# Four small edits of order in an encoder block: fold splits, PSUM bank names, the queue of the residual stores, the place of two means

## The chip, the cores and the metric

The kernel runs on one core of a Trainium2 chip. The metric is device time in microseconds (us), the median of several executions. A core has TensorE (PE: matmuls into PSUM; PEld is its weight load), VectorE (DVE), ScalarE (ACT), GpSimd (POOL) and SyncE (SP), which run their own instruction queues in order and wait for one another by semaphores. Transfers (DMA) are issued from an engine's queue, here nearly all from SyncE's.

## The reference

One encoder block on 1040 positions (16 meta tokens and 1024 inputs), D = 1024, in float32:

```python
h = rmsnorm(h_res, g_mix_pre)
u_a, c_g, b_g, v_b, gate_logits = split(h @ w_in)
y_a = fourier_mix(u_a) @ w_fourier          # real part of a 2-D DFT, 4 groups of 128
y_b = (b_g * centred_dwconv(c_g * v_b)) @ w_conv_out
gates = sigmoid(gate_logits + b_gates)
merged = gates[0] * y_a + gates[1] * y_b
h_res = h_res + rmsnorm(merged @ w_out, g_mix_post)
h2 = rmsnorm(h_res, g_ffn_pre)
a, v = split(centred_dwconv(h2 @ w_up))     # 2 x 2816 columns
h_res = h_res + rmsnorm((gelu(a) * v) @ w_down, g_ffn_post)
return h_res[:, 16:]
```

## The kernel before

**Arithmetic.** Each float32 operand is split into a high part (a cast on ScalarE, L127) and a low part (a subtraction on VectorE, L128). A product is then three matmuls, hi x hi, hi x lo, lo x hi (`mm3`, L155 to L163). Most products are tiled as pairs (`Pair`, L272): two rows of weights times two halves of the sequence in seven products in place of eight, with sums and differences of the operands. The seven steps of a pair use four PSUM tiles a, b, c, d and a sum u in SBUF; step 5 ends with x12 = d + u, step 6 with x21 = c + u (both L144 on VectorE).

**Stages.** In order: the input projection (gates, then the convolution branch, whose last jobs have the tiles `B_a` to `B_d`); the DFT along positions (`pq`, L731: 240 matmuls in eight groups of 30, one per block of 128 channels); the rest of the DFT, the merge and its store to `merged_d`; the output projection `mo` with both norms, in four chunks of 258, 258, 258 and 256 positions; the up projection (`up_*`) with convolution and gate; the down projection (`dna`, `dnb`); the last norm.

**Folds.** The operand of pq, folded by symmetry, has been stored in DRAM as `fold_d`, eight blocks. `next_fold(kt)` (L643) loads block kt into a raw room (`SP.dma_start`, L647) and splits it into `u` tiles. Rooms are shared: blocks 0, 2 and 4 use the raw room "b11h", blocks 1, 3 and 5 "t1l", so block 4 can be loaded only when block 2 is split. Blocks 0 to 3 are fetched from hooks in the last job of the projection, after its steps 1, 2, 4 and 5. Blocks 4 to 7 follow after the stage, then the cosine and sine tables (`cosr`, `sinr`, L738, with casts `cosh`, `sinh`). pq's banks come free with the last job's x21. `yb_d` takes the two results t of that job (L581).

**Output projection.** `project(c, hooks)` makes the eight tiles of chunk c: 24 matmuls each, then a square (`sq_m`, L884) and a scaling (L933) on ScalarE that evict them. Hooks run after numbered tiles, counted from 0. For chunks 1 and 2 (L1160): after tile 1 `norm_a(c - 1)`, after tile 5 `load_merged(c + 1)` (`mr`), after tile 6 `mean_b(c - 1)` and `norm_b(c - 1)`. `norm_a` scales the previous chunk's h by its first norm, adds the residual loaded as `xr` (L951), squares h (`sq_h`, ScalarE), and stores h to `hres_d` (L958), 32 stores in all, which the last stage reads back. `mean_b` is one matmul with a matrix of ones (`ms_h`, L892); `norm_b` scales h in place for the feed-forward (L977) and splits it. For chunk 3 the order of the tiles and the hooks are others (L1162 on), and the up projection's first products (`early`, `plain`) are woven in; `plain.first` copies a product to `up_s` on ScalarE (L1026), and the early pieces of the up projection's weights are loaded as `up_0er` and `up_1er` (L200).

**Order.** There is no table of costs. Instructions come in program order, except that code in `with behind(x):` is placed after instruction x, and each engine keeps that order. PSUM in the down projection is a pool of eight banks; `A` (`dna`) and `B` (`dnb`) are four tiles each, named at L1262, and the first step writes A.

Of the kernel before, what the change touches and what calls it, by code (L numbers as in the profile page):

```python
# [86 lines left out]
def block_kernel(ctx, tc, xT, w_u, w_in, w_fa, w_fa2, w_fb, w_fb2, w_co, w_out, w_up, w_dn,  # L87
# [17 lines left out]
    hres_d = dram.tile([P, KT, NTM], F32, name="hres_d")  # L105
# [13 lines left out]
    V, S, SP = nc.vector, nc.scalar, nc.sync  # L119
# [4 lines left out]
    def split(hi, lo, src, scale=None, eng=V, copy=S.copy):  # L124

        if scale is None:
            a = copy(hi, src)  # L127
            b = eng.tensor_tensor(out=lo, in0=src, in1=hi.bitcast(F32), op=ALU.subtract)  # L128
        else:
            a = S.mul(hi, src, scale)  # L130
            b = V.scalar_tensor_tensor(
                out=lo, in0=src, scalar=scale, in1=hi.bitcast(F32), op0=ALU.mult, op1=ALU.subtract
            )
        return a.ins, b.ins

    def behind(*instructions):

        st = ExitStack()
        for i in instructions:
            st.enter_context(tc.issue_after(i))  # L140
        return st

    def add(out, a, b, eng=V):
        return eng.tensor_tensor(out=out, in0=a, in1=b, op=ALU.add).ins  # L144
# [111 lines left out]
    def whole(t):  # L256
        return t[:, PS0 : PS0 + NH]
# [14 lines left out]
    class Pair:  # L272
# [11 lines left out]
        def step(self, psum, i, w, x):  # L284
            n = self.name
            if i == 0:
                self.a = wtile(psum, f"{n}_a")
                product(self.a, w, x, True, True)
                self.u = self.sums()
                self.kept = S.copy(self.u, whole(self.a)).ins  # L290
            elif i == 1:
                self.d = wtile(psum, f"{n}_d")
                product(self.d, w, x, True, True, self.parts)
            elif i == 2:
                b = wtile(psum, f"{n}_b")
                product(b, w, x, True, True, self.parts)
                add(self.u, whole(b), self.u)
                self.x22 = self.dst(22)
                self.added = add(self.x22, whole(self.d), self.u)
            elif i == 3:  # L300
                self.c = wtile(psum, f"{n}_c")
                product(self.c, w, x, True, True)
                add(self.x22, whole(self.c), self.x22)
                self.done(22, self.x22)
            elif i == 4:
                product(self.a, w, x, False, True)
                self.done(11, whole(self.a))
            elif i == 5:
                product(self.d, w, x, False, True)
                x12 = self.dst(12)  # L310
                add(x12, whole(self.d), self.u)
                self.done(12, x12)
            else:
                product(self.c, w, x, False, True)
                x21 = self.dst(21)
                add(x21, whole(self.c), self.u)
                self.done(21, x21)
# [8 lines left out]
    def run_pairs(psum, jobs, acts, hooks={}, first=None):  # L326

        loads = {0: first}

        def start(n):  # L330
            if n < len(jobs):
                pair, srcs, steps = jobs[n]
                loads[n] = ring.pair(pair.name, *srcs, steps)

        if first is None:
            start(0)
        start(1)
        cur = list(loads[0])
        for n, (pair, _, steps) in enumerate(jobs):
            nxt = []  # L340
            for j, i in enumerate(steps):
                pair.step(psum, i, cur[j], acts[PIECES[i]])
                if i > 1 and n + 1 < len(jobs):
                    todo = -(-len(jobs[n + 1][2]) * (j + 1) // len(steps))
                    with behind(pair.added):
                        nxt += itertools.islice(loads[n + 1], todo - len(nxt))
                if (n, i) in hooks:
                    hooks[n, i]()
            cur = nxt
            start(n + 2)  # L350
# [241 lines left out]
    jobs = []  # L592
# [42 lines left out]
        ("b11h", "b11l", "t1h"), ("t1l", "t2h", "t2l"), ("b11h", "t3h", "t3l"), ("t1l", "b21h", "b21l"),  # L635
        ("b11h", "b22h", "b22l"), ("t1l", "b11l", "t1h"), ("t4h", "b21h", "b21l"), ("t4l", "b22h", "b22l"),
    )
    folded = []

    def room(tag, dt, name):  # L640
        return hxp.tile([P, 4 * NH], dt, tag=tag, name=name)

    def next_fold(kt):  # L643

        raw, hi, lo = (room(t, dt, f"u{kt}{i}") for i, (t, dt) in enumerate(zip(FOLD_ROOMS[kt], (F32, F32R, F32R))))
        w = FW + 512
        SP.dma_start(raw[:, :w], fold_d[kt])  # L647
        split(hi[:, :w], lo[:, :w], raw[:, :w])
        xs = [(hi[:, at : at + H], lo[:, at : at + H]) for at in (H, 0)]
        folded.append((xs, (hi[:, FW:w], lo[:, FW:w])))  # L650

    hooks = {(NE1 + kt, 3): lambda kt=kt: transformed(kt) for kt in range(KT)}
    for kt in range(KT):
        hooks[NE1 + kt, 5 if kt < KT - 1 else 0] = lambda kt=kt: fold(kt)
    hooks[len(jobs) - 1, 1] = lambda: next_fold(0)
    hooks[len(jobs) - 1, 2] = lambda: next_fold(1)
    hooks[len(jobs) - 1, 4] = lambda: next_fold(2)
    hooks[len(jobs) - 1, 5] = lambda: next_fold(3)
    run_pairs(psum, jobs, hx, first=job0, hooks=hooks)
    proj_s.close()  # L660


# [47 lines left out]
    def bank(name):  # L710
        return psum.tile([P, 512], F32, tag="bank", name=name)
# [5 lines left out]
    with ExitStack() as st:  # L717
# [37 lines left out]
        for i in range(NLT):  # L755
            n = _lrows(i)
# [49 lines left out]
    for f in range(KT):  # L806
# [41 lines left out]
        lo = TM - T0 + CHM[1][0]  # L848
# [46 lines left out]
    def load_merged(c):  # L895
        c0, n = CHM[c]
        v = valid(c)
        parts = []
        for k in range(0, KT, 3):
            e = min(k + 3, KT)  # L900
            t = ring.raw(f"mr{c}_{k}")[:, : (e - k) * n].rearrange("p (k n) -> p k n", n=n)
            SP.dma_start(t[:, :, :v], merged_d[:, k:e, c0 + TM - T0 : c0 + TM - T0 + v])
            if v < n:
                V.memset(t[:, :, v:], 0.0)
            parts += [merged_parts(c, kt, t[:, kt - k])[0] for kt in range(k, e)]
        merged[c] = parts
# [32 lines left out]
    def norm_a(c):  # L939
        c0, n = CHM[c]  # L940
        v = valid(c)
        ms = next(z[c])
        rr = np_.tile([P, W], F32, tag="rr", name=f"rr{c}", bufs=2)[:, :n]
        got = rsqrt_of(f"r2_{c}", scratch, ms, n, rr)
        sq = squares(f"h{c}", n)
        next(sq)
        xr = []
        for f in range(0, KT, 2):
            t = eo.tile([P, 2 * W], F32, tag="o", name=f"xr{c}_{f}", bufs=4)
            t = t.rearrange("p (f n) -> p f n", f=2)  # L950
            SP.dma_start(t[:, :, :v], xT[:, f : f + 2, TM + c0 : TM + c0 + v])  # L951
            xr += [t[:, i, :v] for i in range(2)]
        for f in range(KT):
            h = h_at(c, f)
            scaled = mul(h, h, rr).ins
            add(h[:, :v], h[:, :v], xr[f])
            sq.send(h)
            SP.dma_start(hres_d[:, f, c0 : c0 + v], h[:, :v])  # L958
        z[c] = sq
        return got, scaled  # L960

# [7 lines left out]
    def norm_b(c):  # L969
        c0, n = CHM[c]  # L970
        if c not in rs:
            inverse(c)
        rr = rs[c]
        A, B = second(c)
        for f in range(KT):
            h = h_at(c, f)
            V.scalar_tensor_tensor(out=h, in0=h, scalar=col("g_fpre", f), in1=rr, op0=ALU.mult, op1=ALU.mult)  # L977
            if c < 2:
                a, e = max(c0, 1), min(c0 + n, NH + 1)
                put(hx["b11" if f < 4 else "b21"], f % 4, hA[f // 4][:, f % 4, a:e], a - 1, e - a)  # L980
            elif f < 4:
                sub(A(f), h, A(f))
                put(hx["t1"], f, A(f), c0 - 513, n)
            else:
                put(hx["b22"], f - 4, B(f), c0 - 513, n)
# [16 lines left out]
    def mean_b(c):  # L1002
        z[c] = next(z[c])
# [153 lines left out]
    project(0, {4: new_banks, 5: lambda: load_merged(1)})  # L1157
    for c in range(1, 4):
        hooks = {
            1: lambda: norm_a(c - 1), 5: lambda: load_merged(c + 1), 6: lambda: (mean_b(c - 1), norm_b(c - 1)),  # L1160
        }
        order = range(KT)  # L1162
        if c == 3:
            order = (6, 7, 0, 1, 4, 5, 2, 3)
            hooks = {
                1: lambda: norm_a(2),
                3: lambda: plain.load(0, "t1h"),
                4: lambda: plain.load(1, "t1l"),
                5: lambda: first_blocks("t3h"),
                6: lambda: (mean_b(2), inverse(2)),  # L1170
                7: lambda: first_blocks("t3l"),
            }
        project(c, hooks, order)
# [63 lines left out]
    jobs = [ups[n] for n in ORDER]  # L1237
# [21 lines left out]
    z11, u, z22 = (fn.tile([P, 4, HALF], F32, name=n) for n in ("z11", "dn_u", "z22"))  # L1259
    zz = (z11, u), (z12, z22)  # L1260
    ssum = [fn.tile([P, HALF], F32, name=f"ss{i}") for i in range(2)]
    B, A = ([bank(f"dn{n}{f}") for f in range(4)] for n in "ba")  # L1262
    LATE = 4
    AHEAD = 3
    CUT = 256
# [233 lines left out]
```

## Time and profile before

| what | value |
| --- | --- |
| median of 3 runs | 1218.7 us (1218.63 to 1220.26) |
| the profiled execution | 1222.5 us |
| its span | 1220.7 us |
| mean granted TensorE clock in it | 0.986 |
| PE busy | 1186.2 us (97%) |
| DVE busy | 1001.6 us (82%) |
| ACT busy | 550.6 us (45%) |
| DMA moved | 184.01 MB, 151 GB/s in the mean |

Times in the trace are us from the start of the span. Busy time is the time in which an engine executes; issues of transfers, semaphores and branches are not counted. The chain that ended last is followed back from the last instruction, at each step to what released it. A wait is idle time of an engine ahead of an instruction, put down to what released it last. A row of the timeline gives start, duration, engine, line, operation, out<-in with shapes, count, and in brackets the idle time ahead of it. The profile names lines of the kernel before; in the changed kernel, lines below L660 stand 11 further down.

### The profile page before, as it was taken

To read this page: it belongs to the slowest core of one execution; us is meant where nothing else is said; L and a number is where in the kernel's file an instruction comes from. 1 tells how busy PE (TensorE), PEld (TensorE's weight loads), DVE (VectorE), ACT (ScalarE), POOL (GpSimd) and SP (SyncE) were. 2 spreads that over 40 slices of the span, in tenths; PEclk is the share of its full clock that TensorE was granted. 3 is DMA by queue.
4 is the path that set the end of the run, shared out by engine and by line. 5 is a ranking of instruction groups with operands and counts; after the bars stand their busy time and mean duration, and the time that the engine had idled before them with its cause. 6 is when DMAs were issued, how large, how long until landed. Compare 5 with 4: busy or idle time off the path is not lost.

```text
span 1220.7 us, 22312 instructions
## 1 busy us (share of the span) xinstructions
PE 1186.2 (97%) x8822; PEld 1143.0 (94%) x8822; DVE 1001.6 (82%) x1755; ACT 550.6 (45%) x999; POOL 0.4 (0%) x6
## 2 busy tenths in 40 slices
PE   8999999999999999998999999999999999999995
PEld 7999999999999999998999999999999988888884
DVE  8999876757488866989699999989988989766678
ACT  6743333323342344656545443444344434454562
POOL 0000000000000000000000000000000000000000
PEclk9999999999999999999999999999999999999998
DMA  6336554132876757465233334323222498354433
GB/s 248 122 111 219 196 174 165 61 130 85 258 226 216 250 168 116 127 112 152 96 120 123 112 132 147 122 96 130 96 78 87 146 318 313 95 164 121 132 128 138
DMA packets 78472, 184.01 MB, mean 151 GB/s; under 512 B 7934, under 2 KB 24910, under 8 KB 78368
## 3 DMA queue, kind: packets, MB, share of 16 engines
q1 hardware_dynamic: 78224, 182.47, 47.5%
q8 instruction: 69, 1.13, 0.4%
q14 instruction: 35, 0.29, 0.1%
q10 hardware_dynamic: 144, 0.12, 0.0%
HBM read 131.30 MB, written 51.26 MB: 150 GB/s over the span
## 4 chain that ended last, share of the span: by engine, by line
PE 75%; DVE 14%; DMA 7%; issue 2%; ACT 2%; SPq 0%; DVEq 0%; ACTq 0%
PE up_d L159 3%; PE up_d L163 3%; PE up_d L161 3%; PE up_c L161 3%; PE up_c L159 3%; PE dna L159 3%; PE up_c L163 3%; PE dna L161 3%; PE dna L163 3%; PE up_a L159 3%; PE up_a L163 3%; PE up_a L161 3%; PE pq L731 2%; PE dnb L163 2%; PE dnb L161 2%; PE dnb L159 2%
## 5 line engine op out<-in xcount | busy, mean ns | idle before, releaser
L159 PE MATMUL mo<-mh,wo 128*128 128x258 f32 (+1 forms) x256 | 73.9, 289 | 0.0
L163 PE MATMUL mo<-mh,wo 128*128 128x258 f32 (+1 forms) x256 | 73.1, 285 | 0.0
L161 PE MATMUL mo<-ml,wo 128*128 128x258 f32 (+1 forms) x256 | 72.9, 285 | 0.0
L159 PEld LDWEIGHTS mo<-mh,wo 128*128 128x128 f32 x256 | 49.3, 192 | 0.2
L161 PEld LDWEIGHTS mo<-ml,wo 128*128 128x128 f32 x256 | 49.2, 192 | 0.2
L163 PEld LDWEIGHTS mo<-mh,wo 128*128 128x128 f32 x256 | 49.2, 192 | 0.0
L127 ACT CAST up_1h<-up_1t 128x512 fp32r<-128x512 f32 x11 | 6.8, 622 | 75.2 <-DVE up_1t L144 52.5
L1096 ACT ACTIVATE up_1o<-up_1x,pr 128x512 f32<-128x512 f32 x33 | 26.9, 816 | 27.9 <-DVE up_1x L144 27.5
L1100 ACT ACTIVATE up_0o<-up_0o 128x512 f32<-128x512 f32 x44 | 27.8, 631 | 24.1 <-DVE up_0o L1098 23.8
L159 PE MATMUL up_d<-b22h,up_5h 128*128 128x258 f32 (+1 forms) x168 | 34.0, 283 | 0.8 <-DVE up_1x L144 0.8
L163 PE MATMUL up_d<-b22h,up_5l 128*128 128x258 f32 (+1 forms) x168 | 34.2, 284 | 0.0
L161 PE MATMUL up_c<-t3l,up_3h 128*128 128x258 f32 (+1 forms) x168 | 34.1, 285 | 0.0
L163 PE MATMUL up_b<-t2h,up_2l 128*128 128x258 f32 (+1 forms) x168 | 34.0, 283 | 0.0
L161 PE MATMUL up_d<-b22l,up_5h 128*128 128x258 f32 (+1 forms) x168 | 33.9, 283 | 0.0
L161 PE MATMUL up_b<-t2l,up_2h 128*128 128x258 f32 (+1 forms) x168 | 33.9, 283 | 0.0
L159 PE MATMUL up_c<-t3h,up_3h 128*128 128x258 f32 (+1 forms) x168 | 33.8, 282 | 0.0
L159 PE MATMUL up_b<-t2h,up_2h 128*128 128x258 f32 (+1 forms) x168 | 33.8, 282 | 0.0
L159 PE MATMUL up_c<-t4h,up_6h 128*128 128x258 f32 (+1 forms) x168 | 33.8, 282 | 0.0
L159 PE MATMUL up_d<-t1h,up_1h 128*128 128x258 f32 (+1 forms) x168 | 33.7, 282 | 0.0
L163 PE MATMUL up_d<-t1h,up_1l 128*128 128x258 f32 (+1 forms) x168 | 33.7, 282 | 0.0
L163 PE MATMUL up_c<-t3h,up_3l 128*128 128x258 f32 (+1 forms) x168 | 33.6, 281 | 0.0
L161 PE MATMUL up_d<-t1l,up_1h 128*128 128x258 f32 (+1 forms) x168 | 33.6, 281 | 0.0
(1321 smaller groups left out, 4328.4 us busy)
## 6 DMA issues: line engine op xcount, KB each, us to landing
g<-gp_d SPq DMA_DIRECT2D x35, 512.0 KB
up_1r<-in_w_up_dram SPq DMA_DIRECT2D x22, 512.0 KB
gp_d<-up_0o SPq DMA_DIRECT2D x44, 256.0 KB
up_0r<-in_w_up_dram SPq DMA_DIRECT2D x20, 512.0 KB
s<-sig_d SPq DMA_DIRECT2D x16, 514.0 KB
sig_d<-g_s SPq DMA_DIRECT2D x30, 257.0 KB
u<-fold_d SPq DMA_DIRECT2D x8, 777.0 KB
fold_d<-fold SPq DMA_DIRECT2D x8, 521.0 KB
```

The lines of the kernel that those rows point to most:

```text
L127: a = copy(hi, src)
L159: nc.tensor.matmul(o, wh, h, start=first, stop=False, **kw)
L161: nc.tensor.matmul(o, wh, l, start=False, stop=False, **kw)
L163: newest[:] = [nc.tensor.matmul(o, wl, h, start=False, stop=last, **kw).ins]
L731: nc.tensor.matmul(o, a[:, s], b[:, ks], start=kt == n_ == ks.start == 0, stop=kt == KT - 1 and n_ == 2, skip_group_check=True,)
L1096: S.activation(t, ap[:, 1 : 1 + HALF], AF.Identity, bias=col("cb_ffn", b), scale=w(1))
L1100: S.activation(t, t, AF.Gelu_apprx_tanh)
```

## The change

Four edits.

```diff
@@ Pair.step
-                add(x12, whole(self.d), self.u)
+                self.freed = add(x12, whole(self.d), self.u)
@@ folds
-    def next_fold(kt):
+    def load_fold(kt):
...
         SP.dma_start(raw[:, :w], fold_d[kt])
-        split(hi[:, :w], lo[:, :w], raw[:, :w])
...
+        loaded.append((hi[:, :w], lo[:, :w], raw[:, :w]))
+
+    def split_fold(kt):
+        split(*loaded[kt])
+
+    def next_fold(kt):
+        load_fold(kt)
+        split_fold(kt)
...
-    hooks[len(jobs) - 1, 4] = lambda: next_fold(2)
-    hooks[len(jobs) - 1, 5] = lambda: next_fold(3)
+    for step, kt in ((1, 0), (2, 1), (4, 2)):
+        hooks[len(jobs) - 1, step] = lambda kt=kt: next_fold(kt) if kt < 2 else load_fold(kt)
+    hooks[len(jobs) - 1, 5] = lambda: load_fold(3)
     run_pairs(psum, jobs, hx, first=job0, hooks=hooks)
+    with behind(jobs[-1][0].freed):
+        split_fold(2)
+        split_fold(3)
@@ norm_a
-            SP.dma_start(hres_d[:, f, c0 : c0 + v], h[:, :v])
+            S.dma_start(hres_d[:, f, c0 : c0 + v], h[:, :v])
@@ hooks of chunks 1 and 2
-            1: ..., 5: ..., 6: lambda: (mean_b(c - 1), norm_b(c - 1)),
+            1: ..., 5: ..., 7: lambda: (mean_b(c - 1), norm_b(c - 1)),
@@ down projection
-    B, A = ([bank(f"dn{n}{f}") for f in range(4)] for n in "ba")
+    A, B = ([bank(f"dn{n}{f}") for f in range(4)] for n in "ab")
```

The hooks at 1 and 5 (`norm_a`, `load_merged`) stay. What the edits do to the engines' queues is seen at three places.

VectorE at the end of the input projection. `B_s` of B_d is x12, `B_s` of B_c is x21 (which frees pq's banks), the `u` rows are the splits of folds 2 and 3, the `t` rows products of the convolution branch. Before:

```order
409 L128 TENSOR_TENSOR u_3674<-u_3672,u_3673 128x1554
410 L144 TENSOR_TENSOR B_s_3702<-B_d,B_u 128x514
411 L150 TENSOR_TENSOR t_0_3491<-B_s_3702,t_0_3491 128x514
412 L128 TENSOR_TENSOR u_3707<-u_3705,u_3706 128x1554
413 L144 TENSOR_TENSOR B_s_3735<-B_c,B_u 128x514
414 L150 TENSOR_TENSOR t_1_3492<-B_s_3735,t_1_3492 128x514
```

And now:

```order
409 L144 TENSOR_TENSOR B_s_3700<-B_d,B_u 128x514
410 L128 TENSOR_TENSOR u_3674<-u_3672,u_3673 128x1554
411 L150 TENSOR_TENSOR t_0_3491<-B_s_3700,t_0_3491 128x514
412 L144 TENSOR_TENSOR B_s_3731<-B_c,B_u 128x514
413 L128 TENSOR_TENSOR u_3705<-u_3703,u_3704 128x1554
414 L150 TENSOR_TENSOR t_1_3492<-B_s_3731,t_1_3492 128x514
```

Each of the two adds now stands ahead of a split that it stood behind. On SyncE, the store of the second t (`yb_d<-t_1`) now stands ahead of the load of fold 5, behind which it stood.

ScalarE in the output projection of chunk 2, where `norm_a(1)` squares h of chunk 1. Before:

```order
341 L884 ACTIVATE sq_h_3_5539<-hA_5136 128x258 [waits DVE_49,Activation_49]
342 L884 ACTIVATE sq_h_4_5545<-hA_5137 128x258 [waits DVE_49,Activation_49]
343 L884 ACTIVATE sq_h_5_5551<-hA_5137 128x258 [waits DVE_49,Activation_49]
344 L884 ACTIVATE sq_h_6_5557<-hA_5137 128x258 [waits DVE_49,Activation_49]
345 L884 ACTIVATE sq_h_7_5563<-hA_5137 128x258 [waits DVE_49,Activation_49]
346 L884 ACTIVATE sq_m_2_5592<-mo_2_5567 128x258 [waits DVE_49,PE_49]
347 L933 ACTIVATE hA_5136<-mo_2_5567,pr 128x258
```

And now:

```order
346 L895 ACTIVATE sq_h_4_5545<-hA_5137 128x258 [waits DVE_49,Activation_49]
347 L969 DMA hres_d<-hA_5137 128x258 [waits DMAHW7_49]
348 L895 ACTIVATE sq_h_5_5551<-hA_5137 128x258 [waits DVE_49,Activation_49]
349 L969 DMA hres_d<-hA_5137 128x258 [waits DMAHW1_49]
350 L895 ACTIVATE sq_h_6_5557<-hA_5137 128x258 [waits DVE_49,Activation_49]
351 L969 DMA hres_d<-hA_5137 128x258 [waits DMAHW2_49]
352 L895 ACTIVATE sq_h_7_5563<-hA_5137 128x258 [waits DVE_49,Activation_49]
353 L969 DMA hres_d<-hA_5137 128x258 [waits DMAHW4_49]
354 L895 ACTIVATE sq_m_2_5592<-mo_2_5567 128x258 [waits DVE_49,PE_49]
355 L944 ACTIVATE hA_5136<-mo_2_5567,pr 128x258
```

A store stands behind each square, and some of them wait for an earlier transfer's semaphore, ahead of the evictions of the next tiles (`sq_m` and the scaling).

TensorE where the down projection begins, the last row of the up projection and the first of `dna`. Before:

```order
7756 L163 MATMUL up_1_c<-t4h,up_1_6l 128x256
7757 L159 MATMUL dna_12181<-gd_0h,wd_0h 128x512 [waits DVE_49,Activation_49]
7758 L161 MATMUL dna_12181<-gd_0l,wd_0h 128x512
7759 L163 MATMUL dna_12181<-gd_0h,wd_0l 128x512
7760 L159 MATMUL dna_12182<-gd_0h,wd_0h 128x512
```

And now:

```order
7756 L163 MATMUL up_1_c<-t4h,up_1_6l 128x256
7757 L159 MATMUL dna_12177<-gd_0h,wd_0h 128x512 [waits DVE_49,Activation_49]
7758 L161 MATMUL dna_12177<-gd_0l,wd_0h 128x512
7759 L163 MATMUL dna_12177<-gd_0h,wd_0l 128x512
7760 L159 MATMUL dna_12178<-gd_0h,wd_0h 128x512
```

Nothing moves there but the numbers of the tiles; the first row waits for VectorE in both. The matmul of the mean, `ms_h` of chunks 0 and 1, stands 24 rows later on TensorE than before, at the end of the eighth tile instead of the seventh.

More of the change, by code (lines that the diff above doesn't have):

```diff
@@ L637, in block_kernel @@
     )
-    folded = []
+    folded, loaded = [], []
     def room(tag, dt, name):
         return hxp.tile([P, 4 * NH], dt, tag=tag, name=name)
-    def next_fold(kt):
+    def load_fold(kt):
         raw, hi, lo = (room(t, dt, f"u{kt}{i}") for i, (t, dt) in enumerate(zip(FOLD_ROOMS[kt], (F32, F32R, F32R))))
@@ L654, in block_kernel @@
         hooks[NE1 + kt, 5 if kt < KT - 1 else 0] = lambda kt=kt: fold(kt)
-    hooks[len(jobs) - 1, 1] = lambda: next_fold(0)
-    hooks[len(jobs) - 1, 2] = lambda: next_fold(1)
-    hooks[len(jobs) - 1, 4] = lambda: next_fold(2)
-    hooks[len(jobs) - 1, 5] = lambda: next_fold(3)
+    for step, kt in ((1, 0), (2, 1), (4, 2)):
+        hooks[len(jobs) - 1, step] = lambda kt=kt: next_fold(kt) if kt < 2 else load_fold(kt)
+    hooks[len(jobs) - 1, 5] = lambda: load_fold(3)
     run_pairs(psum, jobs, hx, first=job0, hooks=hooks)
+    with behind(jobs[-1][0].freed):
+        split_fold(2)
+        split_fold(3)
     proj_s.close()
@@ L1159, in block_kernel @@
         hooks = {
-            1: lambda: norm_a(c - 1), 5: lambda: load_merged(c + 1), 6: lambda: (mean_b(c - 1), norm_b(c - 1)),
+            1: lambda: norm_a(c - 1), 5: lambda: load_merged(c + 1), 7: lambda: (mean_b(c - 1), norm_b(c - 1)),
         }
```

## The prediction

> **What bounds the kernel now.** I read the profile's page first: busy times, then the chain that ended last by engine.
>
> ```profile
> span 1220.7 us, 22312 instructions
> PE 1186.2 (97%) x8822; PEld 1143.0 (94%) x8822; DVE 1001.6 (82%) x1755; ACT 550.6 (45%) x999; POOL 0.4 (0%) x6
> PE 75%; DVE 14%; DMA 7%; issue 2%; ACT 2%; SPq 0%; DVEq 0%; ACTq 0%
> ```
>
> TensorE is busy for 1186.2 of 1220.7 us, and no edit here removes a matmul. So all that the change can give lies in TensorE's waits and in the time that its clock is held down. The waits, by what ended them, come next (total, times, longest):
>
> ```profile
> PE up_a L159 <- ACT up_u L290: 2.9, 2, 1.9
> PE dna L159 <- DVE up_1x L144: 2.7, 1, 2.7
> PE ms_h L892 <- DVE sq_h L144: 2.4, 1, 2.4
> PE up_z L159 <- ACT up_s L1026: 2.2, 1, 2.2
> PE pq L731 <- DVE B_s L144: 2.1, 1, 2.1
> ```
>
> Each of the four edits points at one of these rows: fold at pq, banks at dna, mean at ms_h, stores at the two rows of the up projection. I then cut the stretches around the waits into windows of 3.41 us and read the granted clock (PEclk):
>
> ```profile
> 312.65:316.06 3.41, 1.28 (x11) 1.24 (x11) 2.86 (x4) 1.49 (x1) 0.00 (x0) 1.00 0.97 304
> 316.06:319.47 3.41, 3.41 (x18) 3.41 (x17) 1.67 (x1) 0.00 (x0) 0.00 (x0) 0.50 0.92 311
> ...
> 575.47:578.88 3.41, 1.55 (x13) 1.35 (x13) 3.38 (x10) 2.76 (x6) 0.00 (x0) 1.00 0.01 4
> 578.88:582.29 3.41, 3.41 (x19) 3.41 (x18) 2.52 (x4) 1.76 (x3) 0.00 (x0) 0.50 0.21 75
> ...
> 991.90:995.31 3.41, 3.38 (x8) 2.73 (x9) 3.41 (x6) 0.73 (x1) 0.00 (x0) 0.50 0.86 315
> ```
>
> The columns are the window, its length, busy time of PE, PEld, DVE, ACT, POOL, the clock, DMA share, GB/s. A window in which TensorE was busy for 1.28 or 1.55 us is followed by one at half clock, worth 3.41 x 0.50 = 1.7 us of work lost. After a shorter wait that does not happen:
>
> ```profile
> 554.98:558.39 3.41, 2.33 (x18) 1.00 0.91 172
> 558.39:561.80 3.41, 2.73 (x23) 1.00 0.51 196
> ```
>
> (only TensorE's busy time here): with 2.33 us busy the next window keeps its clock. So a wait of some 2 us costs about 3.8 us here, and a wait of about 1 us costs only itself. The Trainium skill ("TensorE: Matmul & The Clock Gate", the quick table at its end) asks for no idle gaps over about 3 us; this trace shows half clock after gaps of 1.9 to 2.1 us, so I go by the trace; by the page's figure no gap here would be punished and each edit would be worth its wait alone.
>
> **Fold.** Around the start of pq, in the chain and on VectorE, SyncE's and ScalarE's queues:
>
> ```profile
> 314.85 30.45 PE pq L731 x240
> ...
> 308.24 1.78 DVE L128 TENSOR_TENSOR u<-u,u 128x1554 fp32r<-128x1554 f32 x1 [0.53 <-ACT u L127]
> 309.94 0.69 DVE L144 TENSOR_TENSOR B_s<-B_d,B_u 128x514 f32<-128x514 f32 x1
> 310.66 0.70 DVE L150 TENSOR_TENSOR t<-B_s,t 128x514 f32<-128x514 f32 x1
> 312.32 1.78 DVE L128 TENSOR_TENSOR u<-u,u 128x1554 fp32r<-128x1554 f32 x1 [0.97 <-ACT u L127]
> 315.95 1.78 DVE L128 TENSOR_TENSOR u<-u,u 128x1554 fp32r<-128x1554 f32 x1 [0.51 <-ACT u L127]
> 335.83 1.78 DVE L128 TENSOR_TENSOR u<-u,u 128x1554 fp32r<-128x1554 f32 x1 [1.81 <-ACT u L127]
> ```
>
> ```profile
> 312.33 0.40 PE L163 MATMUL B_c<-t4h,B_6l 128*128 128x258 f32 x2
> ```
>
> The last product ends at 312.73. The add that frees its bank stands behind the split of fold 3 (312.32 to 314.10), so pq starts at 314.85. After the change the add for x12 (309.94, 0.69) comes first, then the split of fold 2 (1.78, to 312.4), the product with t (0.70) and the freeing add (0.69 like its sister): 312.4 + 1.4 = 313.8, or some 0.1 less, since such operations overlap by that much at 309.94. TensorE then starts at about 313.75. The start gains 1.1 us, the remaining gap is 1.0 us, and by the rows above the half-clock window goes too: 1.1 + 1.7 = 2.8 us off, if nothing is late behind it.
>
> Something is. The split of fold 2 now ends at 312.4 instead of 310.0, and its raw room is where fold 4 is loaded. Each load waits in SyncE's queue in order:
>
> ```profile
> 314.13 0.32 SPq L647 DMA_DIRECT2D u<-fold_d  x1
> 317.75 0.73 SPq L738 DMA_DIRECT2D cosr<-in_cos_dram  x1
> ```
>
> cosr goes out at 317.75, right after the split of fold 4 has ended (315.95 + 1.78 = 317.73). A fold 4 loaded 2.3 us later moves this to about 320.0. One store of yb is also now ahead of the load of fold 5 and waits for the second product with t, which stands behind the split of fold 3. ScalarE takes the cosines first:
>
> ```profile
> 330.69 1.50 ACT L127 CAST cosh<-cosr 105x1566 fp32r<-105x1566 f32 x1 [8.83 <-DMA cosr<-in_cos_dram]
> 334.31 2.88 ACT L127 CAST u<-u 128x1554 fp32r<-128x1554 f32 x2
> ```
>
> It idles 8.83 us for cosr, and folds 6 and 7 are cast only after it. pq is eight groups of 30 matmuls; (30.45 - 1.7) / 8 = 3.6 us each. Group 6 began at about 314.85 + 30.45 - 2 x 3.6 = 338.1, and its split ended at 335.83 + 1.78 = 337.6: only 0.5 us of slack. TensorE, 2.8 us earlier, wants group 6 at 335.3. If cosr lands as before, the split holds it to 337.6, a gain of 0.5. If cosr lands 1.2 us (the transfers are bound by the 0.92 to 0.97 DMA share of the windows above, and catch up) to 2.3 us later (they don't), group 6 starts at 338.8 to 339.9, a loss of 0.7 to 1.8; and TensorE's gap there, 2.3 to 4.6 us, may cost another half-clock window, 1.7. Bounds: -0.5 to +3.5. I take the middle, **+1.5**. Without the delay behind it the term would be -2.8.
>
> **Banks.** The chain at the start of the down projection:
>
> ```profile
> 991.18 0.61 DVE up_1x L144
> 991.93 0.76 PE dna L159
> ```
>
> The first dna product waits 2.7 us for the last up_1x add, which reads the bank that the product will write. Swapping the two lists looks as if it gave A other banks. But the banks are handed out when a tile is first written, not when it is named, and A is written first in both programs; in the order of the changed kernel the first dna product waits for VectorE as before. So **0**; both bounds are 0, and the half-clock window at 991.90 stays.
>
> **Stores and mean.** The chain from 478 to 578 is one of VectorE, ScalarE and transfers; TensorE has slack in it. These rows of the chain, and the waits:
>
> ```profile
> 477.97 8.52 DMA mr<-merged_d
> ...
> 499.44 5.52 DMA hres_d<-hA
> ...
> 525.10 15.55 DMA hres_d<-hB
> 540.67 0.49 DVE hB L977
> ...
> 551.73 7.11 DMA up_1er<-in_w_up_dram
> ```
>
> ```profile
> 540.67 0.49 DVE L977 SCALAR_TENSOR_TENSOR hB<-hB,pr,rrb 128x258 f32<-128x258 f32 x1 [3.06 <-DMA hres_d<-hB]
> ```
>
> ```profile
> 544.85 6.34 SPq L958 DMA_DIRECT2D hres_d<-hB  x8
> 551.29 0.38 SPq L1076 DMA_DIRECT2D early_d<-up_1e  x1
> 551.73 0.44 SPq L200 DMA_DIRECT2D up_1er<-in_w_up_dram  x1
> ```
>
> Moving the mean of chunks 0 and 1 one tile later lets 24 matmuls of 0.12 us (3.6 / 30, the same width), 2.9 us, run into the 2.4 us wait of ms_h. That wait is not on the chain: TensorE waits again at the up projection (2.2 and 2.9 above), so time saved at 502 is idled away at 546 to 578. Worth 0 by itself.
>
> The stores leave SyncE's queue. There the last eight stand ahead of the weight load of 551.73, whose landing the chain needs: moved, the load goes out earlier, but still behind the early_d store that waits for ScalarE. Between 0 and -3.0; I take -1.5. VectorE's wait of 3.06 us at 540.67 is for a store to land before its tile is overwritten. The queue changes, the transfer engines don't. Between 0 and -3.06; I take half, -1.5. Against this, ScalarE issues 32 stores. The only issue on its queue now took:
>
> ```profile
> 0.73 0.41 ACTq L111 DMA_DIRECT2D pr<-in_par_dram  x1
> ```
>
> Eight a chunk at 0.41 are 3.3 us, between squares that come as fast as VectorE's adds, so most is hidden; but the copy of up_s for which TensorE waited 2.2 us at the up projection now stands behind five such stores of chunk 3: 0 to +2. VectorE's scaling of chunk 0 (four operations, 1.7 us) also falls behind its wait for mr (8.52 above): 0 to +1.7. Together I take +0.5. Sum **-2.5**, bounds -6 to +4 (the upper end below, under the rival).
>
> The Trainium skill ("Trainium Kernel Development and Optimization", Key Constraints) says that transfers issued by several engines run on the same 16 DMA engines, and that this only saves issue time. By that rule the 3.06 us stay and the term would be -1.0; no run here shows it yet.
>
> **Sum.** +1.5 + 0 - 2.5 = -1.0 us. The profiled execution took 1222.5 us with a span of 1220.7, 3.8 over the median of the runs, 1218.7; the difference is carried to the median: 1217.7.
>
> **Rivals.**
> 1. *The transfers come earlier* (0.36). Stores land sooner beside loads that no longer queue behind them, the 3.06 us at 540.67 and the load at 551.73 are saved in full (-6), and the fold yields between 0 and its -0.5: 1212 to 1214, with the half-clock window of 578.88 gone too 1211. For it: the chain names the transfers. Against: DMA share near full at these places.
> 2. *Slower: ScalarE is blocked by its stores* (0.28). In the changed order the later stores of a chunk wait for DMA semaphores (one for each of eight in rotation), among them those of the xr loads, and behind them stand the evictions of the out projection, a square and a scaling for each tile. If each of chunks 0 and 2 holds ScalarE for 2 us beyond what TensorE's slack covers, +4; with the fold at +1.5 that is 1224. It decides where a wait of a store exceeds the 2.2 us of slack at the next up_z. For it: the order shows the waits; the fold's bound of +3.5 alone, with the stores at 0, gives 1222. Against: ScalarE is busy only 45%.
> 3. *Every named wait goes with its half-clock window* (0.04): -2.8, -(2.7 + 1.7) for banks, -(2.4 + 1.7) for the mean, -3.06: 1204. Against: the order at dna and the slack of group 6.
> 4. *The change does not do what it says*: for the banks that is my forecast already.
>
> **Chances.** My forecast (-1.0, within about 2.4) has 0.32, the rest as above. A measurement of this kernel can tell about 0.2%, 2.4 us, from no change. Rivals 1 and 3 are faster by more, rival 2 slower: faster 0.40, same 0.32, slower 0.28. The range drops rival 3 and the outer parts of 1 and 2: 1211.5 to 1223.5. The forecast's own: 1216.3 to 1221.
>
> **What would show it.** Right: pq starts at 313.7 with a gap near 1.0 and full clock after it, but a new wait of pq on u before its seventh group, with cosr's cast later than 330.69; dna waits 2.7 us as before with half clock behind it; ms_h waits little and the up projection as much or nearly. Wrong: dna starts right after the last up product (banks did move), pq runs through without a wait (the fold is worth -2.8), or ScalarE's waits on DMA stand ahead of the evictions and TensorE waits for mo (rival 2).

## The result and the profile after

The changed kernel took 1227.95 us in the median of 4 runs (1226.38 to 1229.44) against 1218.66 us of the kernel before (1217.15 to 1220.26): ratio 1.0079, 95% interval 1.0063 to 1.0096, so 9.3 us slower. Timed again in another session the ratio was 1.0063 (1.0041 to 1.0086). The forecast was 1217.7, the range 1211.5 to 1223.5. The kernel before itself lies at 1213.6 to 1218.7 in different sessions; so only ratios within a session are compared below, and a ratio is turned into us with 1215.

The page of the changed kernel's profiled execution:

```profile
span 1224.4 us, 22290 instructions
PE 1185.4 (97%) x8822; PEld 1140.8 (93%) x8822; DVE 1002.0 (82%) x1755; ACT 551.0 (45%) x999; POOL 0.4 (0%) x6
PE 74%; DVE 15%; DMA 6%; issue 2%; ACT 2%; SPq 0%; DVEq 0%; ACTq 0%
```

Busy times are as before; the loss is in waits. This execution took 1226.4 us and the profiled one of the kernel before 1222.5, 3.8 over that kernel's median, so the two traces lie only 3.9 us apart and a second trace of each is used below. TensorE's waits (total, times, longest):

```profile
PE up_z L159 <- ACT hB L944: 3.1, 1, 3.1
PE dna L159 <- DVE up_1x L144: 2.6, 1, 2.6
...
PE mo L159 <- ACT mh L127: 1.9, 1, 1.9
PE up_a L159 <- ACT up_u L290: 1.8, 2, 1.6
PE ms_h L903 <- DVE sq_h L144: 1.8, 2, 1.2
...
PE pq L742 <- DVE u L128: 1.4, 1, 1.4
...
PE pq L742 <- ACT u L127: 0.9, 1, 0.9
PE pq L742 <- DVE B_s L144: 0.9, 1, 0.9
...
PE mo L159 <- ACT hB L944: 0.8, 1, 0.8
```

Three of the rows at which the edits aim are as the forecast says. pq waits 0.9 us at its start in place of 2.1, ms_h 1.8 us over two chunks in place of 2.4 in one, dna 2.6 us as before. But new rows stand there: pq waits inside itself (0.9 and 1.4), and TensorE waits for ScalarE's work in the output projection: for the evictions L944 (3.1) and for mh (1.9). pq's three waits, in time:

```profile
313.50 0.34 PE L742 MATMUL pq<-u 128*105 128x260 f32 x1 [0.89 <-DVE B_s L144]
336.15 0.36 PE L742 MATMUL pq<-u 128*105 128x260 f32 x1 [0.91 <-ACT u L127]
337.97 0.49 PE L742 MATMUL pq<-u,u 128*105 128x260 f32 x2 [1.45 <-DVE u L128]
```

What ScalarE did in the output projection is seen in its waits between 460 and 585 us:

```profile
ACT sq_h L895 <- DMA xr<-in_xT_dram: 4.4, 2, 2.6
...
ACT sq_m L895 <- DMA xr<-in_xT_dram: 4.0, 1, 4.0
...
ACT sq_h L895 <- DMA hres_d<-hB: 2.1, 1, 2.1
```

No square reads xr or hres_d. What waits is the store ahead of the square in ScalarE's queue, as the timeline of chunk 2 shows (ACTq rows are issues of transfers):

```profile
525.74 0.42 ACT L895 ACTIVATE sq_h<-hB 128x258 f32<-128x258 f32 x1
527.84 0.33 ACTq L969 DMA_DIRECT2D hres_d<-hB  x1
528.26 0.42 ACT L895 ACTIVATE sq_h<-hB 128x258 f32<-128x258 f32 x1 [2.10 <-DMA hres_d<-hB]
530.04 0.33 ACTq L969 DMA_DIRECT2D hres_d<-hB  x1
530.47 0.42 ACT L895 ACTIVATE sq_h<-hB 128x258 f32<-128x258 f32 x1 [1.78 <-DMA xr<-in_xT_dram]
534.49 0.33 ACTq L969 DMA_DIRECT2D hres_d<-hB  x1
534.86 0.38 ACT L895 ACTIVATE sq_m<-mo 128x256 f32<-128x256 f32 x1 [3.98 <-DMA xr<-in_xT_dram]
```

A store may go out only when the semaphore that it takes is free. In this trace the transfers of ScalarE's and SyncE's queues take eight in rotation, and the records name them: the store at 534.49 takes the one of the load of xr issued at 522.63, which landed at 534.47; the store at 530.04 that of the load issued at 521.28, landed at 530.02; the store at 527.84 that of this chunk's first store (520.96), landed at 527.82. Each goes out 0.02 us after the landing. ScalarE stands still for 2.10 + 1.78 + 3.98 = 7.9 us, and the first eviction of the next tiles comes at 534.86. In chunk 0 it stood for 2.6 us in the same way. A stop in chunk 1 carries another name in the list:

```profile
502.15 0.42 ACT L895 ACTIVATE sq_h<-hA 128x258 f32<-128x258 f32 x1 [0.47 <-DVE hA L144]
503.38 0.33 ACTq L969 DMA_DIRECT2D hres_d<-hA  x1
503.81 0.39 ACT L895 ACTIVATE sq_m<-mo 128x258 f32<-128x258 f32 x1 [1.24 <-PE ms_h L903]
```

The store at 503.38 waits for a load of xr that landed at 503.36; five tiles are then evicted one behind the other, and the casts of mh follow only at 506.94. The clock in the stretch of chunk 1 (window, length, PE busy, clock, DMA share, GB/s):

```profile
503.42:506.83 3.41, 1.34 (x8) 1.00 0.84 177
506.83:510.24 3.41, 2.77 (x12) 0.50 0.48 143
510.24:513.66 3.42, 3.42 (x18) 0.50 0.89 297
```

Two waits of mo close together, for those evictions and for mh (0.8 and 1.9 us in the list), leave 1.34 us of work in a window, and two windows at half clock follow.

### The profile page after: what moved, and what is told of

Same layout as the page of the kernel before. It is cut to its first block, busy times and chain, and to the rows that moved or that the text cites. A ratio compares the mean times of both kernels' runs of the same rounds, so it can differ in the third digit from the quotient of the medians.

```text
span 1224.4 us, 22290 instructions
## 1 busy us (share of the span) xinstructions
PE 1185.4 (97%) x8822; PEld 1140.8 (93%) x8822; DVE 1002.0 (82%) x1755; ACT 551.0 (45%) x999; POOL 0.4 (0%) x6
## 4 chain that ended last, share of the span: by engine, by line
PE 74%; DVE 15%; DMA 6%; issue 2%; ACT 2%; SPq 0%; DVEq 0%; ACTq 0%
PE up_d L159 3%; PE up_d L163 3%; PE up_d L161 3%; PE up_c L161 3%; PE up_c L159 3%; PE dna L159 3%; PE up_c L163 3%; PE dna L163 3%; PE dna L161 3%; PE up_a L159 3%; PE up_a L163 3%; PE up_a L161 3%; PE dnb L161 2%; PE dnb L163 2%; PE dnb L159 2%
## 5 line engine op out<-in xcount | busy, mean ns | idle before, releaser
L161 PE MATMUL up_c<-t4l,up_6h 128*128 128x258 f32 (+1 forms) x168 | 33.6, 282 | 0.0
```

Source lines behind the costliest of these rows:

```text
L161: nc.tensor.matmul(o, wh, l, start=False, stop=False, **kw)
```

## The experiments

Theory A: the stores cost because ScalarE, in order, stands still on their semaphores (a stop). Theory B: the later means cost. Theory C: stores and loads from two queues hinder one another in the transfers. Theory F: the fold edit loses behind pq's start. All kernels are in this table; each ratio is against the kernel before in the same session.

| run | kernel | ratio, 95% interval | us |
| --- | --- | --- | --- |
| e1 | stores alone on ScalarE | 1.0028 (1.0012 to 1.0044) | +3.4 |
| e2, e16 | means alone | 1.0013 (0.9997 to 1.0030), 1.0014 (1.0003 to 1.0025) | +1.6, +1.7 |
| e3 | fold alone | 1.0024 (1.0007 to 1.0041) | +2.9 |
| e4 | changed, stores on GpSimd | 1.0039 (1.0021 to 1.0057) | +4.7 |
| e5 | fold, tables later | 0.9999 (0.9984 to 1.0013) | -0.1 |
| e6 | banks exchanged in earnest | 0.9983 (0.9966 to 1.0000) | -2.1 |
| e7 | two stores a chunk, ScalarE | 1.0068 (1.0042 to 1.0094) | +8.3 |
| e8 | two stores a chunk, SyncE | 1.0069 (1.0051 to 1.0087) | +8.4 |
| e9 | the changed kernel again | 1.0063 (1.0041 to 1.0086) | +7.7 |
| e10 | stores alone on GpSimd | 1.0041 (1.0025 to 1.0057) | +5.0 |
| e11 | e5 and e6 together | 0.9968 (0.9950 to 0.9987) | -3.9 |
| e12 | banks edit alone | 0.9999 (0.9980 to 1.0018) | -0.1 |
| e13 | stores on ScalarE, xr on GpSimd | 1.0001 (0.9990 to 1.0013) | +0.1 |
| e14 | xr on GpSimd | 1.0011 (0.9999 to 1.0023) | +1.3 |
| e15 | changed, means as before | 1.0063 (1.0044 to 1.0083) | +7.7 |
| e17 | changed, xr on GpSimd | 1.0034 (1.0013 to 1.0055) | +4.1 |
| e18 | e11, stores on ScalarE, xr on GpSimd | 0.9973 (0.9951 to 0.9994) | -3.3 |

### The single edits

**e1, stores alone.**

```diff
-            SP.dma_start(hres_d[:, f, c0 : c0 + v], h[:, :v])
+            S.dma_start(hres_d[:, f, c0 : c0 + v], h[:, :v])
```

> The kernel before with the hres stores alone moved to ScalarE's queue; folds, banks and means as before. Theory A (ScalarE stands still in front of its stores, 2.1 + 1.8 + 4.0 us in chunk 2 of the changed kernel, and the evictions behind them come late): nearly the whole loss, +6 to +11 us, with the same waits of ScalarE on xr and hres_d around the third chunk's squares. Theory B (the later means cost it): within 2 us of before. Theory C (the transfers themselves are slower when stores and loads come from two queues): +6 to +11 as well, with landings later than the 541.0 us of before by several us.

It cost 3.4 us, less than the 6 to 11 of theories A and C, since the loss turned out to have more parts. ScalarE's waits on transfers between 460 and 585 us have the new rows:

```profile
ACT sq_h L884 <- DMA xr<-in_xT_dram: 3.4, 1, 3.4
...
ACT sq_m L884 <- DMA xr<-in_xT_dram: 2.4, 1, 2.4
```

A third stop stands under another name: the store at 478.00 goes out 3.4 us after the square ahead of it, and the list puts that to a product of mo. TensorE then waits 2.25 us for mh at 482.46.

**e2 and e16, means alone.**

```diff
-            ... 6: lambda: (mean_b(c - 1), norm_b(c - 1)),
+            ... 7: lambda: (mean_b(c - 1), norm_b(c - 1)),
```

> The kernel before with the means of chunks 0 and 1 alone moved one tile later. Theory A and my forecast: within 2 us of before, the wait of ms_h at 502 gone or below 1 us and the waits at the up projection as long or longer. Theory B (the later means delay norm_b and with it all that follows): +4 to +9 us.

> The later means alone, once more. With the first measurement (+0.13%, interval -0.03 to +0.30%): a cost of 1 to 3 us if it is real, within 1 us of before if it was scatter.

Both times 1.6 to 1.7 us slower, once with an interval that leaves out zero. It is a small cost, not theory B's 4 to 9. Two of TensorE's rows in e16 show what the edit did:

```profile
PE mo L159 <- ACT mh L127: 1.7, 1, 1.7
...
PE ms_h L892 <- DVE sq_h L144: 0.3, 1, 0.3
```

The wait of ms_h (2.4 us in the kernel before, 1.7 in e12) is not removed but moved: with the mean behind the eighth tile, TensorE comes to the next chunk and waits there for the casts of mh, 1.7 us at 504.08 in e16 and 0.6 at 503.98 in e2. All six kept traces with later means have this wait, 0.6 to 1.9 us, and none of the others has one there. That it makes up the 1.6 us is not shown, since the wait of ms_h shrinks by about as much.

**e3, fold alone** (the fold hunk of the change and nothing else).

> The kernel before with the fold edit alone. By the trace of the changed kernel, where pq ended at 345.26 against 345.30 before: within 1 us of before, pq starting near 313.5 and waiting some 2.4 us before its seventh group. Rival: the fold costs some of the 9 us where the trace of one run doesn't show it, +2 to +5.

It cost 2.9 us: the rival was right. The trace of the changed kernel had been a mild case, as the same rows of e3 show, first TensorE's in pq:

```profile
314.49 0.34 PE L742 MATMUL pq<-u 128*105 128x260 f32 x1 [0.89 <-DVE B_s L144]
338.37 0.37 PE L742 MATMUL pq<-u 128*105 128x260 f32 x1 [2.12 <-ACT u L127]
340.18 0.49 PE L742 MATMUL pq<-u,u 128*105 128x260 f32 x2 [1.45 <-DVE u L128]
```

then ScalarE's casts, and the clock after them (columns as above):

```profile
332.45 1.50 ACT L127 CAST cosh<-cosr 105x1566 fp32r<-105x1566 f32 x1 [5.65 <-DMA cosr<-in_cos_dram]
335.43 1.50 ACT L127 CAST sinh<-sinr 105x1566 fp32r<-105x1566 f32 x1 [1.47 <-DMA sinr<-in_sin_dram]
336.83 2.87 ACT L127 CAST u<-u 128x1554 fp32r<-128x1554 f32 x2
```

```profile
340.89:344.30 3.41, 3.41 (x19) 0.50 0.94 260
```

The casts of folds 6 and 7 stand behind those of both tables. pq waits 2.12 + 1.45 us before its seventh group, and a half-clock window follows. Of the six traces with the fold edit and the tables ahead, e3, e4, e15 and e17 have half clock there, the first trace of the changed kernel and e9 have not.

**e12, banks edit alone.**

```diff
-    B, A = ([bank(f"dn{n}{f}") for f in range(4)] for n in "ba")
+    A, B = ([bank(f"dn{n}{f}") for f in range(4)] for n in "ab")
```

> The second edit alone, the two lists of banks named in the other order. A is still written first and still has banks 0, 7, 6, 5: my step says the time is that of before within 0.2%, dna waiting 2 to 2.8 us as before. It also shows how far two kernels with the same instructions lie apart here. Rival: the edit does something after all, over 2.4 us either way.

Nothing, as forecast, and dna waits, 3.3 us, rather longer than the 2 to 2.8 named. Its instructions are those of the kernel before, so its trace is a second execution of that kernel:

```profile
PE dna L159 <- DVE up_1x L144: 3.3, 1, 3.3
```

```profile
DVE hB L977 <- DMA hres_d<-hB: 0.7, 1, 0.7
```

VectorE's wait for a store, 3.06 us in the trace on which the prediction stood, is 0.7 here; in six other traces with eight stores a chunk on SyncE's queue it is 0.6 to 1.9, and e11 has no such row.

### What the stores' move costs

**e4 and e10, the stores on GpSimd's queue**, in the changed kernel and alone.

```diff
-            S.dma_start(hres_d[:, f, c0 : c0 + v], h[:, :v])
+            nc.gpsimd.dma_start(hres_d[:, f, c0 : c0 + v], h[:, :v])
```

> The changed kernel with its hres stores issued from GpSimd's queue, which holds nothing else at that time; all else as changed. Theory A: ScalarE no longer stops, so most of the loss goes: -4 to +2 us against before. Theory C (stores and loads from two queues slow one another): still +6 to +11. If GpSimd's issue is itself slow, VectorE's scaling L988, which waits for the stores to land, is late, and the time lies between.

> The kernel before with the hres stores alone issued from GpSimd's queue. Theory A (the stores' move costs because ScalarE stands still on semaphores ahead of the evictions): GpSimd has nothing behind its stores, so within 1.5 us of before, against +3.4 from ScalarE's queue. Theory C (stores and loads from two queues hinder one another in the transfer engines): +2 to +5 as from ScalarE's.

e4 took 4.7 us over before. That lies between the figures of theory A (-4 to +2) and theory C (+6 to +11); it is what fold and means cost alone (2.9 + 1.6), which theory A's figure had left out. e10 took 5.0 over before, outside theory A's 1.5 and within theory C's +2 to +5. GpSimd has nothing behind its stores; each issue lasts 0.54 us here against 0.33 on ScalarE:

```profile
469.26 0.54 POOL L958 DMA_DIRECT2D hres_d<-hA  x1 [0.28 <-DVE hA L144]
```

The same stores seem to cost 5.0 us alone and next to nothing in e4; the two together decide nothing, and why e10 is slow stays open.

**e7 and e8, two stores a chunk**, on ScalarE's and SyncE's queue.

```diff
-            SP.dma_start(hres_d[:, f, c0 : c0 + v], h[:, :v])
+            if f % 4 == 3:
+                four = hA[f // 4][:, :, c0 : c0 + v] if c < 2 else hB[:, f - 3 : f + 1, c0 - 513 : c0 - 513 + v]
+                S.dma_start(hres_d[:, f - 3 : f + 1, c0 : c0 + v], four)   # e8: SP
```

> The kernel before with the hres stores on ScalarE's queue, two stores of four tiles a chunk in place of eight of one. The same bytes move; a store then seldom meets a semaphore that is still in use. Theory A (the loss of the stores' move is ScalarE standing still on those semaphores): the 3.4 us of loss go, -3 to +1 us against before. Theory C (transfers on two queues hinder one another): still +2 to +5.

> The control to the kernel with two stores a chunk on ScalarE's queue: the kernel before, stores left on SyncE's queue, two of four tiles a chunk in place of eight. If fewer stores alone make the difference, this is as much faster as the other, -3 to 0 us; if the queue matters once ScalarE no longer stops, it stays within 1.5 us of before and the other is faster.

Both expectations fell: 8.3 and 8.4 us slower, on either queue. The stops did go in e7, but for one wait of 0.6 us on xr. VectorE overwrites h in `norm_b` and must wait for the store; a store of four tiles goes out only behind the last of them. VectorE's wait in e7 and in e8:

```profile
DVE hB L979 <- DMA hres_d<-hB: 3.9, 1, 3.9
```

```profile
DVE hB L979 <- DMA hres_d<-hB: 5.7, 1, 5.7
```

As the loss is the same on both queues, these two say nothing on theory A. The late landing is the likely cause; that it is the whole of the 8 us is not shown.

**e13 and e14, the loads of xr on GpSimd's queue**, with the stores on ScalarE's (e13) and on SyncE's (e14). GpSimd's transfers take semaphores of their own (eight others in e13's trace), so a store on ScalarE meets no load of xr.

```diff
-            SP.dma_start(t[:, :, :v], xT[:, f : f + 2, TM + c0 : TM + c0 + v])
+            nc.gpsimd.dma_start(t[:, :, :v], xT[:, f : f + 2, TM + c0 : TM + c0 + v])
```

> The kernel before with the hres stores on ScalarE's queue and the loads of xr issued from GpSimd's. A store on ScalarE then waits for no load of xr. Theory A (ScalarE's stops are the cost): no waits of sq_h or sq_m on a transfer of xr, and the time within 1.5 us of the control with the stores on SyncE. Theory C (stores from another queue than SyncE's cost in the transfers): 2 to 5 us slower than the control.

> The control: the kernel before with the loads of xr issued from GpSimd's queue, stores on SyncE's as before. Theory C says that here, too, stores and loads come from two queues: 2 to 5 us slower than before. Theory A: within 1.5 us of before.

e13 lies at 1.0001: on ScalarE's queue the stores cost nothing once they don't wait for loads. All of ScalarE's waits on transfers between 460 and 585 us in e13:

```profile
ACT mh L127 <- DMA mr<-merged_d: 4.6, 1, 4.6
ACT up_1e_0h L127 <- DMA up_1er<-in_w_up_dram: 3.3, 1, 3.3
ACT ep L127 <- DMA up_1er<-in_w_up_dram: 1.1, 1, 1.1
ACT up_0h L127 <- DMA up_0r<-in_w_up_dram: 0.4, 1, 0.4
```

No square waits for xr. Stores that go out more than 0.35 us after the square ahead of them are late by 8.3 us in sum in e1 and by 9.7, 7.5 and 10.3 in the changed kernel, e9 and e15; e13, e17 and e18, with xr on GpSimd's queue, have none. Theory C wanted e13 2 to 5 us slower than its control; it is 1.2 us faster than e14, and its interval against before ends at 1.6 us. (e14's own reaches 2.8 us, so that a small cost of loads from GpSimd is not excluded.) Theory A stands for ScalarE's queue. The Trainium skill ("Trainium Kernel Development and Optimization", Key Constraints) says that transfers issued by several engines share the same DMA engines and only issue time is saved; e13, which neither gains nor loses, agrees.

**e17, the changed kernel with only that wait taken out** (the same edit).

> The changed kernel with the loads of xr issued from GpSimd's queue, nothing else. If ScalarE's stops on those loads are the stores' whole cost, what is left is fold (+2.9) and means (+1.6): +2.5 to +5.5 us against before, in place of the +7.6 to +9.3 of the changed kernel. If the stops are not the cost in this company: +7 to +9.5.

+4.1 us, within the 2.5 to 5.5 named: the stops make up some 3.6 to 5.5 of the loss of 7.7 to 9.6, and fold and means (2.9 + 1.6) the rest. Runs of different sessions are compared here, each with an error of some 2.6 us.

**e9 and e15, the changed kernel again, and without the later means.**

> The changed kernel itself once more, timed beside the single edits on one chip. If the parts found alone (stores +3.4, fold +2.9, means +1.6) simply add: +8 us against before, within 6 to 11.

> The changed kernel with the means of chunks 0 and 1 back behind their seventh tile. If the later means cost 1.6 us or more in the company of the other edits: +5 to +6.5 us against before, in place of +7.6 to +9.3, and the wait of mo on mh near 505 shorter than its 1.9 us. If they cost nothing: +7 to +9.5.

The single parts sum to 3.4 + 2.9 + 1.6 = 7.9, and e9 found 7.7. e9's trace has chunk 1's stop, the two waits of mo (1.1 and 1.9) and the two half-clock windows at 506.8 again; the 3.1 us wait of up_z behind chunk 2's stops is 0.2 there, so what one stop costs changes from execution to execution. From its first to its last product mo takes 102.9 and 101.2 us in the two traces of the changed kernel, 98.5 and 96.6 in those of the kernel before; pq takes 31.5 and 32.0 in place of 30.1 and 30.2.

Taking the means out again gave nothing (both 1.0063). In e15's trace the wait for mh near 505 is gone, as expected, but mo waits 2.2 us for mh at 486.66, behind two longer stops in chunk 0 (5.9 us, where e9 has 3.0). So the means' 1.6 us show alone and not in company of the other edits; whether a stop takes their place each time was not shown.

### What the edits could have been

**e5, the tables behind fold 7.**

```diff
-        cos_p = table_parts(cos_r, "cos", COS_ROOMS)
-        sin_p = table_parts(sin_r, "sin", SIN_ROOMS)
+        with behind(*fold_done):
+            cos_p = table_parts(cos_r, "cos", COS_ROOMS)
+            sin_p = table_parts(sin_r, "sin", SIN_ROOMS)
```

> The fold edit alone, and the casts and splits of the cosine and sine tables put behind the split of fold 7, so that folds 6 and 7 no longer wait for the tables. Theory F (the fold edit loses because pq, started 1.1 us earlier, waits 2.4 to 3.6 us before its seventh group for casts that stand behind the tables' casts, and then runs a half-clock window): the waits inside pq go, pq ends near 342.3 in place of 345.3, and the kernel is 1 to 4 us faster than before, 3 to 6 faster than with the fold edit alone. Rival G (the loss of the fold edit lies elsewhere, in the later loads or the store of yb): still 1 to 4 us slower than before. Rival H: pq ends earlier, but the first DFT waits as much longer for the tables; then the time is that of before within 1 us.

The chain of e5 has pq in one piece, without a wait, at full clock:

```profile
312.76 28.94 PE pq L742 x240
```

The waits inside pq are gone, and only the order of the casts differs from e3: that part of theory F is shown. The kernel is as fast as before (interval -1.9 to +1.6 us), 3.0 better than e3 across sessions, with an error of some 2.7. Theory F's gain of 1 to 4 us against before is not seen; the time is rival H's, though the trace doesn't show that rival's later wait: mo starts 87.3 us after pq's last product, 87.1 in the trace before. Two things can hide a gain. The traced run of e5 took 1210.96, 2.4 under its median. And the half-clock window that makes 30.45 out of some 28.9 does not always come in the old order of the folds: 8 of its 11 traces have it, e6, e13 and e16 do not. In e6 pq waits 2.1 us as before, but the wait falls into two windows, with 2.17 and 2.58 us of work, and pq takes 28.96 us.

**e6, other banks for A.**

```diff
-    dn_s, psum = scope("psum5", 8, space=PSUM)
+    dn_s, psum = scope("psum5", 4, space=PSUM)
+    psum_a = new_pool(dn_s, "psum5a", 4, space=PSUM)
...
-    B, A = ([bank(f"dn{n}{f}") for f in range(4)] for n in "ba")
+    B = [bank(f"dnb{f}") for f in range(4)]
+    A = [psum_a.tile([P, 512], F32, tag="bank", name=f"dna{f}") for f in range(4)]
```

> The kernel before with the banks of the down projection exchanged in earnest: A and B come from two pools of four banks, so that A takes banks 4, 7, 6, 5 and B 0, 3, 2, 1 (before: A 0, 7, 6, 5 and B 4, 3, 2, 1). The first product of A then waits for the last operation on a and d of the last pair, no longer for x21. If the wait of 2.7 us and the half-clock window behind it are real costs: 2 to 5 us faster than before. If the operands of the next products are late anyway (VectorE is busy 3.38 of 3.41 us there): within 1 us of before, with new waits in the first groups of dna.

2.1 us faster (the interval, 0.9966 to 1.0000, just reaches no change), at the lower end of the 2 to 5 named, and the wait of dna is gone from TensorE's list. Its first rows:

```profile
PE up_a L159 <- ACT up_u L290: 2.6, 1, 2.6
PE ms_h L892 <- DVE sq_h L144: 2.4, 2, 1.4
...
PE pq L731 <- DVE B_s L144: 2.1, 1, 2.1
```

**e11, both; e18, both with the stores on ScalarE and xr on GpSimd.**

> The fold edit with the tables behind fold 7 together with the real exchange of the banks of the down projection; stores on SyncE and means as before. If both are independent: 1 to 6 us faster than before (0 from the first, 2.1 from the second as measured alone, up to 3 from the trace of the first). If what pq gains is lost again in the waits of the output and up projection: 0 to 2 faster, no more than the banks alone.

> All edits as repaired: folds split as in the change, with the tables behind fold 7; banks exchanged in earnest; stores on ScalarE's queue with the loads of xr on GpSimd's; means as before. Against the version with repaired folds and banks and the stores on SyncE (-3.9 us): the same within 1.5 us, since stores on ScalarE without the stops neither cost nor gain; -5.5 to -2 against before.

e11 is the fastest kernel here, 3.9 us under the kernel before (interval 1.6 to 6.1) and by that 11.6 to 13.5 under the changed one across sessions. e18, 3.3 us under before, is the same within the error: stores on ScalarE neither gain nor cost when nothing stops them.

## Why the prediction was wrong, point by point

**Fold, +1.5 (bounds -0.5 to +3.5): mechanism right, size too small.** pq started at 313.50 with a gap of 0.9 (forecast 313.75 and 1.0) and without a half-clock window, and then waited before its seventh group for casts behind the tables, as said. Alone it measured +2.9, within the bounds. The middle of the bounds was taken; the half-clock window behind the new wait, named there as possible, came in four of six traces. The 1.7 us for the window at pq's start were read from one execution and counted as sure, though it comes in 8 of 11.

**Banks, 0: right.** e12 shows it, and e6 shows what the exchange would have been worth: 2.1 us, less than the 2.7 + 1.7 of rival 3.

**Stores and mean, -2.5 (bounds -6 to +4): the step that failed.** The prediction took half of VectorE's 3.06 us and half of the 3.0 of the weight load as gains, and +0.5 for all that ScalarE pays. Measured were +3.4 for the stores, with +1.6 for the means; the sum of the two, 5.0, lies beyond the upper bound. Three things were wrong in it. VectorE's gain was read from one execution, 3.8 us over the median: the wait does go in the traces of the changed kernel and of e1, but in e12, with the instructions of before, the 3.06 are 0.7, so there was little to win. The weight load did not go out earlier: it stands behind the early_d store, which waits for ScalarE, and went out at 558.81 in the changed kernel, 554.21 in e9 and 553.54 in e1, in place of 551.73 and, in e12, 550.97. And the price of ScalarE's issues was worked out from their length (3.3 us a chunk, mostly hidden), though the order showed that some of them wait for semaphores; the wait, up to 4.0 us for a single store, is what counts. Rival 2 had the place and the mechanism, and a time of 1224 with a chance of 0.28; it should have been the forecast. Even it put 2 us on each of chunks 0 and 2, beyond TensorE's slack, where the trace has stops of 2.6 and 7.9 before the slack is taken off, and left out chunk 1.

**Mean, 0 by itself: nearly.** Alone it cost 1.6 to 1.7 us, under what a single measurement tells. That the 2.4 us wait of ms_h was off the chain is right: it shrank, a wait for mh came in its place, and nothing was won.

**The rivals.** Rival 1 (earlier transfers) fell, rival 3 too; rival 1's own terms give 1212.1 to 1212.7, not up to 1214. Rival 4, that an edit does not do what it says, was right for the banks.

## What to carry to other kernels

A transfer issued from a computing engine's queue can be a wait in that queue. Read in the order which semaphore each issue waits for, find in the trace when the transfer that holds it lands, and charge that time to what stands behind it; the length of the issue is the smaller part. A wait that an edit is to remove, or a half-clock window, should be looked for in a second execution before it is counted as a gain, and a start made earlier is worth only as much as the slack of the next operand: ask for it group by group.

## What was not expected of the hardware

Two waits of under 2 us can fall in one 3.41 us window and bring two half-clock windows (1.34 us of work, then 0.50 twice). It goes by the work left in a window, and so by where a wait falls: cut into windows in step with their half-clock windows, between 30 and 1195 us, the 20 kept traces have half clock after every window at full clock with at most 1.55 us of work, after none with more than 1.95, and either in between. A wait of 2.3 us at dna in e1 left 2.47 and 2.09 us in two windows and no half clock followed; 2.0 us in e16 left 1.41 in one, and it did. A second half-clock window came only where TensorE waited within the first (2.30 to 2.93 us of work), and not each time. Stores from GpSimd's queue, with nothing behind them, cost 5.0 us alone (e10) where the same stores from ScalarE without stops cost 0.1 (e13, with xr on GpSimd's queue); no run here tells why.
